# Who forms the sums of a seven-product scheme: accumulating transfers, GpSimd or VectorE, and in which order the pairs come

## The chip, the cores and the metric

One core of a Trainium2 chip runs one layer of a decoder. The metric is device time in microseconds (us) of one execution; the figure for a kernel is the median of several runs.

## The reference, cut to what matters

```python
D_MODEL = 2048; SEQ = 256; N_META = 16; D_FF = 5632      # T = 272 positions
u = rms_norm(h, ffn1_norm_g);  h = h + 0.5 * swiglu(u, w_gate, w_up, w_down)
u = rms_norm(h, mix_norm_g);   z = u @ w_in               # q k v q_idx k_idx w_idx x_c B C gate_attn gate_conv
y_attn = dsa_sparse_attention(q, k, v, q_idx, k_idx, w_idx, k_sel) @ w_attn_branch
y_conv = (gate_b * causal_depthwise_conv(gate_c * x_c, conv_w, conv_b)) @ w_conv_branch
merged = sigmoid(gate_attn) * y_attn + sigmoid(gate_conv) * y_conv
h = h + merged @ w_out
u = rms_norm(h, ffn2_norm_g);  h = h + 0.5 * swiglu(u, w_gate2, w_up2, w_down2)
return h[:, N_META:]
```

All inputs are float32. The kernel gets float32 accuracy by splitting each operand into a high and a low part and multiplying three times (high by high, high by low, low by high).

## The kernel before

**The weight stream.** Every weight is read once from HBM, in the order of use, by the class `Stream`. `load` (L131) issues the transfers on SyncE's queue (SP) into tiles `raw` of 128x2048 floats (1 MB). `split` (L163) cuts a load into subs of at most 128x1024: ScalarE copies a sub into its high part `whi` (L181), VectorE subtracts to get the low part `wlo` (L182). TensorE takes the blocks by `next` (L203). Each time TensorE's program enters a new sub, `next` does four things in this order, and so lays down the order of the instructions on every engine: the `early` functions that are due, the split of the sub that lies `ahead` places further on (3 places in the gates, 5 in the second FFN), the `later` functions that are due (a lag of n means n - 1 subs later), and then the products. There are 3 `raw` tiles up to and with the gates, 4 in the second FFN (`widen`, L124). A `raw` tile can be loaded again when its last sub has been split.

**The stages.** First FFN (to about 790 us of the profile), the mixer's projections, attention and convolution (to about 1086 us), the gates with the two branch products (`gates`, 1086 to 1400), the output projection with `w_out` (1400 to 1478), the second FFN (1478 to the end). The change touches the last three.

**Seven products for eight.** In the gates and in the second FFN, tokens are the stationary side (two blocks of 128 tokens) and 512 weight columns move. A *pair* is two blocks of 128 rows of the sum against two blocks of 512 columns. A pair of kind C is done plainly: eight products of three matmuls each (24 matmuls). A pair of kind S is done as Strassen's method does it: seven products (21 matmuls) into eight PSUM banks `q1` to `q8`, each a 128x512 tile, from sums of weights and sums of tokens. Lists of letters such as `KINDS = "SCSCSCCC"` say which of the eight pairs of a group are C and which are S; a second list says which pair it is.

- Weight sums of an S pair. The five column blocks of a load lie in HBM as a21, a21, a11, a22, a12. SP loads the first two and the next two into one `raw` (L140, L141). GpSimd (POOL) then issues an accumulating transfer that adds a11 and a22 onto the first two (L142), which gives `sa` = (a21 + a11, a21 + a22). The fifth block goes into the small tile `last` (L144; two of these). VectorE forms `sb` in two additions of 128x512 (L159, L160) from `raw` and `last`, in `sum_ahead`, one sub before the pair's first split. The subs of an S pair are "one" (a11, a22), `sa`, `sb`, `last`, of 2, 2, 2 and 1 blocks.
- Token sums of an S pair. `sums_into` (L579) forms four blocks of 128x128 with four instructions on GpSimd; `split_into` (L385) splits the result on ScalarE and VectorE. In the second FFN's down half these are sums of `mid` (tile `more`); `turn_mid` (L1191) puts them, with their split, three lags behind.
- `group` (L617) runs a list of pairs. After the last S pair, `recombine` (L630) puts q1, q5, q6, q7 together in the tiles `va`, `vv`, `vx`, `ve`: one ScalarE copy and four VectorE instructions of 128x512; in a down group four more add the results to `ht` (`after_seven`, L1283). After the last pair, `after_end` adds q3, q2, q4, q8 in that order (L1252 or L1283). A bank can be written by the next group only when its reader here is done. Both come through `early`, so they stand ahead of the splits in VectorE's queue.

**The second FFN's order.** `PLAN` runs four up groups, a down group, four up groups, a down group, three up groups, a down group. An up group makes 512 columns of gate and up. The next group turns its result (`turn_mid`, eight transposes and their split). A down group runs its pairs twice, once for each half of the output columns. So there are eight changes from up group to up group, three from an up to a down group, three from first to second half, and two from a down group to an up group. In up group 0, `norm2` and `turn_h` (transposes of the residual) stand at pair 6.

**Queues.** Each engine's queue is in order. On POOL's queue lie, in the gates and the second FFN, the accumulating transfers, the token sums and some additions of squares (L414).

## Time and profile before

| | |
|---|---|
| median of 3 runs | 2279.72 us (2275.02 to 2285.24) |
| the profiled execution | 2283.87 us; its span from first to last instruction 2282.1 us |
| TensorE busy | 2168.8 us, 95% of the span |
| VectorE busy | 1483.5 us, 65% |
| ScalarE busy | 1085.1 us, 48% |
| GpSimd busy | 125.9 us, 6%, 161 instructions |
| mean granted TensorE clock | 0.979 of full speed |
| HBM read | 439.94 MB |

Times inside the profile count from the first instruction. "Idle before, and what ended it" is given in square brackets behind an instruction; a row of the table of waits gives the total, how often, and the longest. "PEclk" is the share of full clock that TensorE was granted. SPq and POOLq are the queues on which SyncE and GpSimd issue transfers.

### The profile page before, as it was taken

The numbers are of one execution on the slowest core, as the hardware profiler recorded it, in microseconds if no ns is written. First come the engines' busy times: TensorE is split into PE (matmuls) and PEld (weight loads), VectorE is DVE, ScalarE is ACT, GpSimd is POOL, SyncE is SP. The second block draws the span as 40 slices with busy tenths as digits, with TensorE's granted clock in tenths as the row PEclk, the third lists the DMA queues.
The fourth block names the chain that finished last, engine by engine and source line by source line (L and its number), as shares of the span: only waits on it lengthen the run. The fifth ranks groups of instructions, "written<-read, shape, count | busy, mean of one in ns | idle before, by whom it ended". The sixth has DMA issues, their size and how long they took to land. (4 is left out here: it accounts for less than half of the span.)

```text
span 2282.1 us, 32260 instructions
## 1 busy us (share of the span) xinstructions
PE 2168.8 (95%) x13045; PEld 1939.5 (85%) x13045; DVE 1483.5 (65%) x1865; ACT 1085.1 (48%) x1397; POOL 125.9 (6%) x161
## 2 busy tenths in 40 slices
PE   8999999999999999999988999989989999899998
PEld 8999999999999998899866778877767777677776
DVE  7555544555555566875766666777767877678776
ACT  6444433344444454654544444655544555454553
POOL 2000000000000000000200000200000000000010
PEclk9999999999999999999999999999999999999999
DMA  6554555545545545444666654677658776687754
GB/s 240 192 173 178 184 171 181 182 171 183 178 175 184 173 174 170 153 143 166 222 195 192 212 189 169 216 229 226 217 180 251 243 218 215 191 246 239 232 193 139
DMA packets 82517, 444.13 MB, mean 195 GB/s; under 512 B 9184, under 2 KB 9312, under 8 KB 43072
## 3 DMA queue, kind: packets, MB, share of 16 engines
q1 hardware_dynamic: 73584, 410.55, 50.6%
q0 software_dynamic: 8640, 31.35, 8.4%
q8 instruction: 102, 1.67, 0.3%
q14 instruction: 47, 0.39, 0.0%
q10 hardware_dynamic: 144, 0.17, 0.0%
HBM read 439.94 MB, written 2.10 MB: 194 GB/s over the span
## 5 line engine op out<-in xcount | busy, mean ns | idle before, releaser
L182 DVE TENSOR_TENSOR wlo<-raw,whi 128x1024 fp32r<-128x1024 f32 (+1 forms) x752 | 907.8, 1217 | 599.1 <-ACT whi L181 582.9
L181 ACT ACTIVATE whi<-raw 128x1024 fp32r<-128x1024 f32 (+1 forms) x752 | 786.8, 1051 | 868.2 <-PE q L559 185.9
L557 PE MATMUL q<-whi,act 128*128 128x512 f32 x833 | 336.3, 404 | 31.6 <-DVE vx L1252 23.0
L558 PE MATMUL q<-wlo,act 128*128 128x512 f32 x833 | 334.0, 401 | 21.7 <-DVE wlo L182 21.6
L559 PE MATMUL q<-whi,act 128*128 128x512 f32 x833 | 332.4, 399 | 0.0
L557 PEld LDWEIGHTS q<-whi,act 128*128 128x128 f32 x833 | 161.6, 194 | 70.6 <-DVE vx L1252 25.9
L558 PEld LDWEIGHTS q<-wlo,act 128*128 128x128 f32 x833 | 162.3, 195 | 59.3 <-DVE wlo L182 26.0
L351 PE MATMUL pd<-mid,whi 128*128 128x272 f32 x704 | 201.7, 286 | 0.0
L352 PE MATMUL pd<-mid,whi 128*128 128x272 f32 x704 | 201.7, 286 | 0.0
L353 PE MATMUL pd<-mid,wlo 128*128 128x272 f32 x704 | 201.7, 286 | 0.0
L351 PE MATMUL pg<-act,whi 128*128 128x272 f32 x672 | 192.7, 287 | 0.0
L353 PE MATMUL pg<-act,wlo 128*128 128x272 f32 x672 | 192.5, 287 | 0.0
L352 PE MATMUL pg<-act,whi 128*128 128x272 f32 x672 | 192.5, 286 | 0.0
L351 PE MATMUL pu<-act,whi 128*128 128x272 f32 x672 | 192.5, 286 | 0.0
L352 PE MATMUL pu<-act,whi 128*128 128x272 f32 x672 | 192.5, 286 | 0.0
L353 PE MATMUL pu<-act,wlo 128*128 128x272 f32 x672 | 192.5, 286 | 0.0
L559 PEld LDWEIGHTS q<-whi,act 128*128 128x128 f32 x833 | 161.7, 194 | 34.6
L557 PE MATMUL q<-whi,mid 128*128 128x512 f32 x272 | 112.0, 412 | 38.1 <-DVE va L1252 23.9
L351 PEld LDWEIGHTS pd<-mid,whi 128*128 128x128 f32 x704 | 132.6, 188 | 0.0
L352 PEld LDWEIGHTS pd<-mid,whi 128*128 128x128 f32 x704 | 132.6, 188 | 0.0
L353 PEld LDWEIGHTS pd<-mid,wlo 128*128 128x128 f32 x704 | 132.6, 188 | 0.0
L352 PEld LDWEIGHTS pg<-act,whi 128*128 128x128 f32 x672 | 126.6, 188 | 0.0
(286 smaller groups left out, 3792.9 us busy)
## 6 DMA issues: line engine op xcount, KB each, us to landing
raw<-in_wgu_dram SPq DMA_DIRECT2D x87, 1024.0 KB, 4.8
raw<-in_w_dram SPq DMA_DIRECT2D x84, 1024.0 KB, 5.0
raw<-in_w2s_dram SPq DMA_DIRECT2D x96, 512.0 KB, 5.3
raw<-in_wd_dram SPq DMA_DIRECT2D x44, 1024.0 KB, 4.8
raw<-in_wcv_dram SPq DMA_DIRECT2D x24, 1024.0 KB, 4.8
raw<-in_w2s_dram POOLq DMA_DIRECT2D x48, 512.0 KB, 5.8
raw<-in_wg_dram SPq DMA_DIRECT2D x21, 1024.0 KB, 5.9
raw<-in_wb_dram SPq DMA_DIRECT2D x16, 1024.0 KB, 4.8
```

The source lines that it names most:

```text
L181: nc.scalar.activation(to[0], raw, AF.Copy)
L182: nc.vector.tensor_sub(to[1], raw, to[0].bitcast(F32))
L351: nc.tensor.matmul(ps, whi, xhi, start=first, stop=False)
L352: nc.tensor.matmul(ps, whi, xlo, start=False, stop=False)
L353: nc.tensor.matmul(ps, wlo, xhi, start=False, stop=last)
L557: nc.tensor.matmul(ps, xhi, whi, start=n == 0, stop=False)
L558: nc.tensor.matmul(ps, xhi, wlo, start=False, stop=False)
L559: nc.tensor.matmul(ps, xlo, whi, start=False, stop=n == total - 1)
```

## The change

1. Gates: kind S now loads four blocks (a21, a11, a22, a12) in one transfer of 1 MB. VectorE forms `sa` itself in one addition of 128x1024 and then `sb` as before. No accumulating transfer is left there. The gates' groups after the first run their pairs in the order C S S C S C C C (`pairs_gate`).
2. Second FFN: the pairs with an accumulating transfer stay, as kind D. `last` gets three tiles. Down groups run C C D C D C D C (before C C S C S S C C) and C C D C D C (before C C S S C C).
3. Both kinds: the subs come as `sa`, `sb`, one, `last`; the products as q7, q5, q6, q3, q1, q4, q2 (before q1, q4, q7, q5, q6, q3, q2).
4. Token sums are three VectorE instructions in place of four on GpSimd, and sum and split lie at lags of their own (2 and 3, or 3 and 5).
5. `after_end` in the second FFN adds q3, q4, q2, q8. In up group 0, `norm2` and `turn_h` move from pair 6 to pairs 0 to 2; `turn_mid` in a down group uses banks q6 and q1.
6. The pool `tmp` moves to the side that is given back when the residual is.

```diff
-KINDS = "SCSCSCCC"
+KINDS = "DCDCDCCC"
-FIRST = "CCCSCSCC"
+SEVEN = (3, 5, 7)
+def pairs_gate(c):
+    return list(zip("CCCSCSCC", range(PAIRS)) if c == 0 else zip("CSSCSCCC", [0, 3, 5, 1, 7, 2, 4, 6]))
 def pairs_down(gs):
-        kinds, at = "CCSCSSCC", [(0, 2), (1, 2), (0, 0), (2, 2), (1, 0), (2, 0), (3, 0), (3, 2)]
+        kinds, at = "CCDCDCDC", [(0, 2), (1, 2), (0, 0), (2, 2), (1, 0), (3, 0), (2, 0), (3, 2)]
-        kinds, at = "CCSSCC", [(0, 2), (1, 2), (0, 0), (1, 0), (2, 0), (2, 2)]
+        kinds, at = "CCDCDC", [(0, 2), (1, 2), (0, 0), (2, 0), (1, 0), (2, 2)]
...
-            (g, "one", 2 * WIDE, 2, WIDE), (g, "sa", 0, 2, WIDE), (g, "sb", 0, 2, WIDE), (g, "last", 0, 1, WIDE)
+            (g, "sa", 0, 2, WIDE), (g, "sb", 0, 2, WIDE), (g, "one", at * WIDE, 2, WIDE), (g, "last", 3 * WIDE, 1, WIDE)
...
-                last = self.sum_pool.tile([P, WIDE], F32, name="last", tag="last", bufs=2)
+                last = self.sum_pool.tile([P, WIDE], F32, name="last", tag="last", bufs=3)
...
     def sum_ahead(self):
+                if self.seven[g]:
+                    sa, one, last = raw[:, : 2 * WIDE], raw[:, 2 * WIDE : 3 * WIDE], self.sums[g, "last"]
+                else:
+                    add(sa, (raw block 1, raw block 2), (raw block 0, raw block 0))
-                self.nc.vector.tensor_add(sb[:, :WIDE], raw[:, WIDE : 2 * WIDE], raw[:, 2 * WIDE : 3 * WIDE])
-                self.nc.vector.tensor_add(sb[:, WIDE:], sb[:, :WIDE], self.sums[g, "last"])
+                add(sb[:, :WIDE], sa[:, WIDE:], one)
+                add(sb[:, WIDE:], sb[:, :WIDE], last)
...
     def sums_into(t, x):
-        nc.gpsimd.tensor_sub(t[:, 0, :], x[:, 0, :P], x[:, 0, P:])
-        nc.gpsimd.tensor_sub(t[:, 1, :], x[:, 0, P:], x[:, 1, P:])
-        nc.gpsimd.tensor_add(t[:, 2, :], x[:, 1, P:], t[:, 0, :])
-        nc.gpsimd.tensor_sub(t[:, 3, :], x[:, 1, :P], t[:, 2, :])
+        nc.vector.tensor_sub(t[:, :2, :], x[:, 0, :].rearrange("p (j t) -> p j t", j=NT), x[:, :, P:])
+        nc.vector.tensor_add(t[:, 2, :], x[:, 1, P:], t[:, 0, :])
+        nc.vector.tensor_sub(t[:, 3, :], x[:, 1, :P], t[:, 2, :])
...
     def turn_mid(tags):
-            def sums():
-                sums_into(t, x)
-                split_into(two[:, 0, :], two[:, 1, :], t)
-            st.later(sums, 3)
+            st.later(lambda: sums_into(t, x), 3)
+            st.later(lambda: split_into(two[:, 0, :], two[:, 1, :], t), 5)
...
-                    ("q1", b11), ("q4", t4), ("q7", t3), ("q5", t1), ("q6", t2), ("q3", b22), ("q2", b21)
+                    ("q7", t3), ("q5", t1), ("q6", t2), ("q3", b22), ("q1", b11), ("q4", t4), ("q2", b21)
...
-            for tag in ("q3", "q2", "q4", "q8"):
+            for tag in ("q3", "q4", "q2", "q8"):
...
     def up_group(g):                      # g == 0
-                if n >= 6:
-                    for i in range(3) if n == 6 else range(3, 8):
-                        turn_h(i // 2, i % 2, ("q7", "q6", "q5", "q1")[(i - n + 6) % 4 if n > 6 else i])
+                if n < 3:
+                    for i, tag in zip(((0, 1), (2, 3, 4, 5), (6, 7))[n], ("q1", "q5", "q6", "q7")):
+                        turn_h(i // 2, i % 2, tag)
```

## The prediction

> **What bounds the kernel now.** I read the mean clock and the page's busy shares first: TensorE is the bound, so only its stops and its slow stretches can be won. Then I asked for the busy time by stretch, the gates and the second FFN apart, and for TensorE's waits in each.

> ```profile
> 1086.00:1400.00 314.00, 290.58 (x1280) 236.22 (x1279) 200.03 (x223) 148.82 (x171) 19.04 (x24) 0.97 0.60 194
> 1478.00:2283.00 805.00, 725.99 (x3115) 593.77 (x3113) 597.68 (x675) 401.91 (x456) 60.00 (x83) 0.95 0.70 215
> ```

> Length, then busy time of TensorE, weight load, VectorE, ScalarE and GpSimd; then granted clock, share of the DMA engines, GB/s. VectorE has 114 us free in the gates and 207 in the FFN. TensorE's waits (total, times, longest), the two largest of the gates, then five of the FFN:

> ```profile
> PE q L558 <- DVE wlo L182: 18.6, 7, 4.0
> PE q L557 <- DVE va L1131: 3.9, 3, 1.3
> ```
> ```profile
> PE q L557 <- DVE va L1252: 23.9, 3, 10.8
> PE q L557 <- DVE vx L1252: 23.0, 7, 4.8
> PE q L557 <- DVE ht L1283: 18.6, 5, 5.5
> PE pht L1233 <- DVE vx L635: 4.8, 1, 4.8
> PE q L558 <- DVE wlo L182: 3.0, 2, 2.2
> ```

> So 22.5 us of stops in the gates and 73.3 in the FFN. In the FFN 15 of 18 stand at a change of group (L1252, L1283): the first matmul waits for a bank that `after_end` has not emptied. A stop costs clock as well:

> ```profile
> 1774.00:1777.00 3.00, 3.00 (x10) 2.40 (x9) 2.97 (x5) 1.19 (x2) 0.00 (x0) 0.66 0.80 113
> 2170.00:2180.00 10.00, 10.00 (x46) 8.29 (x45) 6.53 (x6) 5.83 (x6) 0.00 (x0) 1.00 0.55 210
> 2203.00:2208.00 5.00, 5.00 (x13) 3.88 (x12) 1.77 (x2) 1.66 (x3) 0.00 (x0) 0.50 0.21 64
> ```

> At full clock 44 whole matmuls take 10 us, 0.227 each (two of the 46 are cut by the edges); behind a stop the clock is 0.50 to 0.66. A C pair is thus 24 x 0.227 = 5.45 us, a seven-product pair 21 x 0.227 = 4.77, one product 0.68. The FFN has 3024 wide matmuls by its loops, 686 us; with some 13 us of transposes and 73.3 of stops, 805 leaves about 32 us lost to low clock, 1.8 for each of 18 stops. In the gates 0.03 x 314 = 9 us is the bound.

> **Part 1: token sums leave GpSimd's queue.** Here is the first change from up to down group, POOL's queue first, then VectorE's, then TensorE:

> ```profile
> 1673.82 0.86 POOL L142 DMA_DIRECT2D raw<-in_w2s_dram  x1 [7.01 <-issue]
> 1674.38 0.78 POOL L582 TENSOR_TENSOR vm<-vm 128x128 f32<-128x128 f32 x1
> ```
> ```profile
> 1666.95 1.22 DVE L182 TENSOR_TENSOR wlo<-raw,whi 128x1024 fp32r<-128x1024 f32 x1 [0.25 <-ACT whi L181]
> 1677.20 0.69 DVE L387 TENSOR_TENSOR more<-vm,more 128x512 fp32r<-128x512 f32 x1 [9.03 <-ACT more L386]
> 1677.81 0.68 DVE L1252 TENSOR_TENSOR vv<-q,vv 128x512 f32<-128x512 f32 x1
> ```
> ```profile
> 1679.24 0.76 PE L557 MATMUL q<-whi,mid 128*128 128x512 f32 x1 [10.76 <-DVE va L1252]
> ```

> An accumulating transfer waits for the plain transfer it adds onto; the token sums stand behind it on POOL, the split of those sums on VectorE waits for them, `after_end` stands behind that split, and TensorE waits for `after_end`. VectorE was free at 1668.17 and TensorE stopped at 1668.48. With the change nothing on VectorE waits for POOL but the weight sums. The three new instructions (one 128x256, two 128x128) have the 128x256 addition as nearest row:

> ```profile
> L182 DVE TENSOR_TENSOR wlo<-raw,whi 128x1024 fp32r<-128x1024 f32 x738 | 898.1, 1227 | 588.5 <-ACT whi L181 576.3 <-PE po L368 0.5
> ...
> L159 DVE TENSOR_TENSOR sb<-raw 128x512 f32<-128x512 f32 x59 | 40.5, 687 | 58.0 <-DMA raw<-in_wgs_dram 46.3 <-DMA raw<-in_w2s_dram 8.6 <-issue 3.0
> ...
> L383 DVE TENSOR_TENSOR h<-h,u 128x256 f32<-128x256 f32 x16 | 6.8, 426 | 8.1 <-ACT u L382 8.1
> ```

> Halving the width from 512 to 256 takes off 0.26, so 128x128 lies between 0.16 and 0.43; I take 0.3, 1.0 us for three, 14 times, 14 us of VectorE's spare time. It counts only ahead of `after_end`.

> *Up to up* (8 changes). `after_end` can start about 0.7 behind TensorE's end (1668.17 + 1.0 against 1668.48), and each of its instructions takes 0.61 back to back. A D pair now comes first and begins with q7, q5, q6, which `recombine` freed pairs ago: nine matmuls, 2.05 us. q3 is then ready at 1.3, q4 at 1.9 (used from 3.4), q2 at 2.5 (from 4.1). No stop, with 0.7 us to spare; the cover is the nine matmuls. The row L1252 `vx` goes, 23.0 us.

> *Up to down* (3). The group begins with C, and C needs q2, which the new order adds third: 0.7 + 3 x 0.61 and a restart of 0.1 to 0.2 are 2.6 us each, 7.8 for 23.9.

> *Up group 0.* The transposes at pairs 0 to 2 use banks that nothing holds, so the 4.8 goes; their cost on TensorE is the same, their eight ScalarE copies lie beside C pairs (ScalarE is 402 of 805 us busy; without that cover the first split of the FFN would be late by them). They also give the second accumulating transfer more time, so the longer of the two waits for L182, 2.2, goes. At the start some 1.2 stays (0.8 of this row and a 0.4 that the view has further down).

> **Part 2: the down groups.** This is VectorE from the last S of a first half, and TensorE's restart:

> ```profile
> 1714.29 0.68 DVE L634 TENSOR_TENSOR vv<-q,va 128x512 f32<-128x512 f32 x1
> ...
> 1719.34 2.35 DVE L182 TENSOR_TENSOR wlo<-raw,whi 128x1024 fp32r<-128x1024 f32 x2
> 1722.70 0.69 DVE L159 TENSOR_TENSOR sb<-raw 128x512 f32<-128x512 f32 x1 [1.00 <-DMA raw<-in_w2s_dram]
> ...
> 1724.04 2.35 DVE L182 TENSOR_TENSOR wlo<-raw,whi 128x1024 fp32r<-128x1024 f32 x2
> 1726.31 2.48 DVE L1283 SCALAR_TENSOR_TENSOR ht<-q,ht 128x512 f32<-128x512 f32 x4
> ```
> ```profile
> 1727.73 0.76 PE L557 MATMUL q<-whi,mid 128*128 128x512 f32 x1 [4.17 <-DVE ht L1283]
> 1773.67 0.50 PE L557 MATMUL q<-whi,act 128*128 128x512 f32 x1 [2.19 <-DVE ht L1283]
> ```

> TensorE stopped at 1723.56; two C pairs (10.9) before that the last S ended, at 1712.66. `recombine` began 1.63 later and ran with `after_seven` for 5.05; four splits (4.6), the next sums (1.34) and 1.0 of waiting follow, then `after_end`. In the new order only one C pair stands behind the last D. In *first to second half* (3), 1.63 + 5.05 + two splits 2.3 + sums 1.34 = 10.3 against 5.45 of cover: `after_end` starts 4.9 late, q2 is third (1.85), and with 0.2 to restart (1727.73 against two additions from 1726.31) the stop is 6.9 each, 20.7 in all, where it is now 4 to 5.5. This step goes against the change. In *down to up* (2), 1.63 + 5.05 + 1.75 (a split of 512, one of 1024) - 5.45 = 3.0, q3 at 3.6 against nine matmuls: 1.7 each where the second row has 2.19. At the very end `recombine` finishes 1.2 behind TensorE and four additions follow, 2.5 us more than now.

> FFN: now 73.3 + 32 = 105; then 1.2 + 7.8 + 20.7 + 3.4 = 33.1 of stops, 8 x 1.8 + 0.5 = 15 of clock, 2.5 at the end: 51. Gain 54. Bounds of this step: every boundary as now but without the waits for POOL gives 60, halves at 9 each give 45. The third `last` tile frees only SP's queue, `tmp` on the other side moves no instruction, and `turn_mid`'s new banks are free since `recombine`: I give these nothing, as no stop is charged to them. The two token sums of the output projection (2 us) lie beside its matmuls.

> **Part 3: the gates.** Issues with KB each and median time to landing, and VectorE's wait there:

> ```profile
> raw<-in_wg_dram SPq DMA_DIRECT2D x21, 1024.0 KB, 5.9
> ...
> raw<-in_wgs_dram SPq DMA_DIRECT2D x22, 512.0 KB, 4.1
> ...
> raw<-in_wgs_dram POOLq DMA_DIRECT2D x11, 512.0 KB, 7.5
> ```
> ```profile
> DVE sb L159 <- DMA raw<-in_wgs_dram: 46.3, 11, 6.4
> ```

> An S pair's sums need 4.1 and then 7.5; after the change one transfer of 5.9, with two issues fewer on SP's queue, none on POOL's, and 0.75 MB less to move. With three `raw` tiles that is the wait of 4.2 a pair behind L182's 18.6. The added 128x1024 addition is 1.23 by the row of `wlo` (between 0.69 and 1.23 by width), 11 times, 14 us of the 114 free. On the path: two S pairs in a row need 2 x (2.6 of sums + 4.1 of splits) = 13.4 on VectorE against 9.5, behind the merge's six instructions (3.7) and with a C pair (5.45) of lead. Through the queue from TensorE's entry into the group: merge to 3.7, two splits to 6.0, the second S's sums to 8.6, the first S's 512-wide split to 9.2. Only then is its tile loaded for the third S: landed at 15.1, summed at 17.7, and the C split behind that at 18.9, which TensorE wants at 17.7 (C, S, S and half a C). So 1.2 stays for each of three groups. C first uses q2 and q3, free since the branch, so the wait for the merge (L1131, 3.9) goes. Gates: 22.5 + 9 becomes 4 + 1.5, gain 26.

> **Sum.** 54 + 26 = 80. The profiled execution is 2283.87, 4 us above the median of the runs, well within their spread: 2204 against it, 2200 for the median.

> [...] In the row from 1774 the clock fell behind a stop of 2.19. [...]

> [...]

> [...]

> **The rivals.**
> - *VectorE's queue takes half of it back* (0.20). `after_end` starts a split later than I have it (1.2 us, over the spare 0.7) at the eight up changes, and the gates keep half of their stops. 8 x (0.5 to 1.5 + 1.8) = 18 to 26, plus 13: 2231 to 2239. For it: VectorE's work per group does not shrink.
> - *Less is left than I have it* (0.08). If sums and splits at the halves run ahead of `recombine`, 3 x 3.6 come off, 2189; if short stops cost no clock, 9 come off, 2191; both 2180. Against it: the order of the program, and the row from 1774.
> - *GpSimd only looked guilty* (0.08): behind it VectorE's own backlog holds `after_end`, as at 1726.31. The FFN stays, only the gates' 26 are won, the halves lose 8: 2262.
> - *Slower* (0.06): `sa` is first in a D pair, so the accumulated half is wanted two products (1.36 us) earlier. If each of the 48 transfers is just in time now, that is 65 us of stops, and at 1 us of clock each (half of what a stop costs now, as they are short) 48 more: 2200 + 113 = 2313. It decides from 1.7 us a pair (80 / 48). Against it: the sums, which stand ahead of all subs in VectorE's queue, need the same half already, and only 8.6 us of their wait (L159) is charged to these transfers.

> **How the numbers follow.** The forecast has 0.58, 2186 to 2222 by itself. The range takes in the first two rivals: 2178 to 2243. No change is within 0.5%, 11 us. Faster: 0.58 + 0.20 + 0.08 and half of the third, 0.90; same 0.05; slower 0.05.

> **What would show it.** The waits for L1252 `vx` and L1131 gone; VectorE never waiting for `more`; three stops of about 7 us at the changes of half and three near 2.6 into a down group; FFN clock 0.97 to 0.98; gates near 287 us. I am wrong if VectorE waits for `raw` in most D pairs, or if the up groups keep stops over 1 us.

## The result, and the profile after

The changed kernel takes 2196.88 us (median of four runs, 2194.66 to 2201.74) beside 2277.37 us for the kernel before: a ratio of 0.9644, 95% interval 0.9612 to 0.9676. Its profiled execution took 2201.74 us, the longest of the four, with a span of 2200.0, so the span is 82.1 us shorter.

Where the time went is cleanest between three marks: the first matmul of the gates, the first of the second FFN, the end. From the timeline, TensorE (start, length, line, operation), before and then after:

```profile
1086.76 0.40 PE L557 MATMUL q<-whi,act 128*128 128x512 f32 x1
1470.21 0.40 PE L557 MATMUL q<-whi,act 128*128 128x512 f32 x1
```
```profile
1086.60 0.40 PE L577 MATMUL q<-whi,act 128*128 128x512 f32 x1
1436.47 0.40 PE L577 MATMUL q<-whi,act 128*128 128x512 f32 x1
```

Gates and output projection went from 383.5 to 349.9 us, 33.6 won; the second FFN, to the end of the span, from 811.9 to 763.5, 48.4 won. The stages before the gates are unchanged. By the matmuls the projection starts at 1378.03 and the FFN at 1470.21 in the kernel before, not at 1400 and 1478; all of the 33.6 lies in the gates, as the projection takes 92.2 us in both kernels. Busy time by stretch after the change, columns as in the prediction (the first stretch holds the gates and the start of the projection, the second the FFN without its first 8.5 us):

```profile
1086.00:1400.00 314.00, 311.88 (x1461) 260.26 (x1460) 238.35 (x279) 167.12 (x205) 3.85 (x4) 1.00 0.54 190
1445.00:2201.00 756.00, 709.52 (x3108) 583.25 (x3106) 599.94 (x700) 395.63 (x454) 41.05 (x47) 0.97 0.74 229
```

In the gates TensorE is busy 311.88 of 314 us at full clock, where it had 290.58 at 0.97. VectorE does more there (238.35 for 200.03) and it does not matter. TensorE's waits after the change, those of the FFN and then the only two left in the gates and the projection:

```profile
PE q L577 <- DVE ht L1301: 23.9, 5, 6.8
PE q L577 <- DVE va L1270: 9.4, 3, 4.2
...
PE q L577 <- DVE vv L1270: 4.1, 2, 2.7
PE pht L1251 <- ACT ht L1252: 2.5, 1, 2.5
```
```profile
PE po L386 <- ACT whi L202: 1.3, 2, 0.7
PE q L578 <- DVE wlo L203: 0.8, 1, 0.8
```

`after_end` is now L1270 (up) and L1301 (down), the split L202 and L203. The row `vx` (23.0 us in seven waits) is gone. The FFN's stops are 40.3 us with one of 0.4 that the rows above leave out, where they were 73.7 (73.3 and one of 0.4). One of each kind, in order of time:

```profile
1575.78 0.50 PE L577 MATMUL q<-whi,act 128*128 128x512 f32 x1 [1.42 <-DVE vv L1270]
1619.05 0.47 PE L577 MATMUL q<-whi,mid 128*128 128x512 f32 x1 [2.62 <-DVE va L1270]
1670.09 0.76 PE L577 MATMUL q<-whi,mid 128*128 128x512 f32 x1 [6.83 <-DVE ht L1301]
1717.50 0.50 PE L577 MATMUL q<-whi,act 128*128 128x512 f32 x1 [1.69 <-DVE ht L1301]
1847.42 0.50 PE L577 MATMUL q<-whi,act 128*128 128x512 f32 x1 [2.67 <-DVE vv L1270]
2119.36 0.77 PE L577 MATMUL q<-whi,mid 128*128 128x512 f32 x1 [4.19 <-DVE va L1270]
```

The first and the fifth are two of the three stops left at a change from up to up group (the third is the one of 0.4, for a copy on ScalarE); the second and the sixth stand into a down group; the third is a change of half (three of them, 6.83 each), the fourth a change from down to up (two, 1.69 each).

### The profile page after: what moved, and what is told of

Same layout as the page of the kernel before. It is cut to its first block, busy times and chain, and to the rows that moved or that the text cites. A ratio compares the mean times of both kernels' runs of the same rounds, so it can differ in the third digit from the quotient of the medians.

```text
span 2200.0 us, 32155 instructions
## 1 busy us (share of the span) xinstructions
PE 2143.0 (97%) x13045; PEld 1926.7 (88%) x13045; DVE 1503.8 (68%) x1918; ACT 1080.3 (49%) x1397; POOL 82.3 (4%) x94
## 4 chain that ended last, share of the span: by engine, by line
PE 85%; DVE 8%; ACT 2%; DMA 2%; issue 1%; POOL 1%; SPq 0%; DVEq 0%; ACTq 0%; POOLq 0%
PE q L577 11%; PE q L578 11%; PE q L579 11%; PE pd L372 4%; PE pd L371 4%; PE pd L373 4%; PE pu L371 4%; PE pg L371 4%; PE pg L373 4%; PE pu L373 4%; PE pu L372 4%; PE pg L372 4%; DVE wlo L203 3%; DMA raw<-in_w2d_dram 2%; ACT whi L202 2%; PE po L386 1%
## 5 line engine op out<-in xcount | busy, mean ns | idle before, releaser
L203 DVE TENSOR_TENSOR wlo<-raw,whi 128x1024 fp32r<-128x1024 f32 (+1 forms) x752 | 903.7, 1208 | 607.5 <-ACT whi L202 591.2
L202 ACT ACTIVATE whi<-raw 128x1024 fp32r<-128x1024 f32 (+1 forms) x752 | 782.8, 1044 | 858.8 <-PE q L579 187.8
L577 PE MATMUL q<-whi,act 128*128 128x512 f32 x833 | 327.1, 393 | 8.0 <-DVE vv L1270 4.1
L578 PE MATMUL q<-wlo,act 128*128 128x512 f32 x833 | 325.5, 391 | 0.8 <-DVE wlo L203 0.8
L579 PE MATMUL q<-whi,act 128*128 128x512 f32 x833 | 325.0, 390 | 0.0
L577 PEld LDWEIGHTS q<-whi,act 128*128 128x128 f32 x833 | 157.0, 188 | 42.5 <-DVE vv L1270 5.4
L578 PEld LDWEIGHTS q<-wlo,act 128*128 128x128 f32 x833 | 157.0, 188 | 33.6 <-DVE wlo L203 1.9
L579 PEld LDWEIGHTS q<-whi,act 128*128 128x128 f32 x833 | 156.9, 188 | 32.9
## 6 DMA issues: line engine op xcount, KB each, us to landing
raw<-in_wgu_dram SPq DMA_DIRECT2D x87, 1024.0 KB, 4.8
raw<-in_w_dram SPq DMA_DIRECT2D x84, 1024.0 KB, 5.0
raw<-in_w2d_dram SPq DMA_DIRECT2D x96, 512.0 KB, 5.5
raw<-in_wd_dram SPq DMA_DIRECT2D x44, 1024.0 KB, 4.8
raw<-in_wg_dram SPq DMA_DIRECT2D x32, 1024.0 KB, 4.8
raw<-in_wcv_dram SPq DMA_DIRECT2D x24, 1024.0 KB, 4.8
raw<-in_w2d_dram POOLq DMA_DIRECT2D x48, 512.0 KB, 5.7
raw<-in_wb_dram SPq DMA_DIRECT2D x16, 1024.0 KB, 4.9
```

What stands on the lines that cost most here:

```text
L202: nc.scalar.activation(to[0], raw, AF.Copy)
L203: nc.vector.tensor_sub(to[1], raw, to[0].bitcast(F32))
L577: nc.tensor.matmul(ps, xhi, whi, start=n == 0, stop=False)
L578: nc.tensor.matmul(ps, xhi, wlo, start=False, stop=False)
L579: nc.tensor.matmul(ps, xlo, whi, start=False, stop=n == total - 1)
```

## The experiments

Ratios are to the kernel before, measured beside each run on the same chip. Beside these runs it took 2275.4 to 2280.6 us (medians), so a difference of a few us between two runs is at the edge of what their times alone can tell.

### Token sums: is it the engine or the place?

The change does two things to the token sums of the down groups: it moves them from GpSimd to VectorE, and it takes their split from the lag of the sums (3) to a later one (5), which puts that split behind `after_end` in VectorE's queue. Each was undone alone, then both.

e1, the sums back on GpSimd, the lags as changed:

```diff
-        nc.vector.tensor_sub(t[:, :2, :], x[:, 0, :].rearrange("p (j t) -> p j t", j=NT), x[:, :, P:])
-        nc.vector.tensor_add(t[:, 2, :], ...); nc.vector.tensor_sub(t[:, 3, :], ...)
+        nc.gpsimd.tensor_sub(t[:, 0, :], x[:, 0, :P], x[:, 0, P:])   # and the other three, as before
```

> Token sums back on GpSimd (four instructions), everything else as changed: the split of the sums still lies two subs behind them. Queue theory (TensorE stops because after_end stands in VectorE's queue behind a split that waits for POOL's queue): that split now stands behind after_end, so nothing is held; stops from up to up group as in the changed kernel or smaller (VectorE has 1.0 us less ahead of after_end), 2190 to 2202 us. Rival (GpSimd itself is too slow or too late for these sums): VectorE waits for `more` again by some 4 us eight times, 2225 to 2240 us.

e2, the sums on VectorE, with their split at lag 3:

```diff
-            st.later(lambda: split_into(two[:, 0, :], two[:, 1, :], t), 5)
+            st.later(lambda: split_into(two[:, 0, :], two[:, 1, :], t), 3)
```

> Token sums on VectorE, but sum and split at the same lag, as before the change, in the second FFN's down half. Queue theory: the split's VectorE half waits about 1 us for ScalarE and takes 0.6, all ahead of after_end: stops near 1 us appear at the eight changes from up to up group, and those into a down group grow by 1.6; 2208 to 2220 us. Rival (only the engine matters): no change, 2194 to 2200.

e3, both edits:

> Token sums on GpSimd and sum and split at the same lag: the whole token-sum part undone, the orders kept. Queue theory: VectorE's wait for `more` returns (about 30 us in all), the stops into a down group return to about 10, 10 and 3 us, those from up to up group to 1.5 to 2.5 us, less than before because q7, q5, q6 come first; 2232 to 2252 us. Rival (the order of products alone cured the changes of group): 2197 to 2212.

| sums on | split behind `after_end` (lag 5) | split ahead of it (lag 3) |
|---|---|---|
| VectorE | 2196.88, 0.9644 [0.9612, 0.9676] (the change) | 2210.61, 0.9694 [0.9676, 0.9712] (e2) |
| GpSimd | 2190.49, 0.9606 [0.9585, 0.9626] (e1) | 2228.0, 0.977 [0.9751, 0.9789] (e3) |

The place decides more than the engine. Putting the split late is worth 13.7 us with the sums on VectorE and 37.5 with them on GpSimd. The engine is worth 17.4 us with the split early, where VectorE waits for GpSimd as before. With the split late GpSimd's queue costs nothing here, and the sums on VectorE are if anything 6 us dearer (the two intervals overlap). In e2, as expected, VectorE waits 0.7 us for `more` at eight places and the stops into a down group are 4.00 each, where the regular ones of the change are 2.62; of the eight changes from up to up, five stop, for 0.68 to 2.94. e3 has the old chain again, in small. VectorE's total wait for `more` there, then from the timeline POOL, VectorE, and TensorE's restart at a change from up to up group:

```profile
DVE more L407 <- ACT more L406: 25.0, 8, 4.6
```
```profile
1583.09 0.86 POOL L149 DMA_DIRECT2D raw<-in_w2d_dram  x1 [9.09 <-DVE wlo L203]
1583.65 0.79 POOL L602 TENSOR_TENSOR vm<-vm 128x128 f32<-128x128 f32 x1
...
1586.50 0.69 DVE L407 TENSOR_TENSOR more<-vm,more 128x512 fp32r<-128x512 f32 x1 [3.40 <-ACT more L406]
...
1587.85 0.50 PE L577 MATMUL q<-whi,act 128*128 128x512 f32 x1 [2.40 <-DVE vv L1271]
```

The sums start on POOL only behind the issue of a transfer, VectorE idles 3.40 us for their split, and `after_end` starts behind it, at 1587.11. In e1, with the sums in the same queue, one wait for `more` of 1.0 us is left, and it stands behind `after_end`. e3 came 4 us better than the lower end of what was expected: its stops into the down groups were 4.28, 4.28 and 4.69, not 10, 10 and 3. Its five stops from up to up were 1.87 to 4.39, longer than the 1.5 to 2.5 expected.

e1's stops at the changes of group are also smaller than the change's: into a down group 5.4 us for 9.4 and from up to up 0.2 for 4.5. Its stops at the FFN's start are longer by 2.9 (two for a split, 1.3, and the transposes' wait for ScalarE 4.1 for 2.5), so in sum 34.9 us stay of 40.3. So the three additions on VectorE are not hidden where `after_end` is already late; the sizes are worked out under "Up to up" below.

In e1 the four sums, all of one shape, differ on GpSimd by more than half in their mean (the slowest and the quickest in the FFN; count, then busy time in us and mean in ns):

```profile
L603 POOL TENSOR_TENSOR vm<-vm 128x128 f32<-128x128 f32 x9 | 10.2, 1137 | 0.0
...
L605 POOL TENSOR_TENSOR vm<-vm,vm 128x128 f32<-128x128 f32 x9 | 6.2, 689 | 0.7
```

No run here shows why, and in e1, with the split late, it cost nothing that the times show (2190.49 us for the change's 2196.88).

### Order of products and subs

e4, the change with the products as q1, q4, q7, q5, q6, q3, q2, the subs as one, `sa`, `sb`, and `after_end` as q3, q2, q4, q8 again:

```diff
-                    ("q7", t3), ("q5", t1), ("q6", t2), ("q3", b22), ("q1", b11), ("q4", t4), ("q2", b21)
+                    ("q1", b11), ("q4", t4), ("q7", t3), ("q5", t1), ("q6", t2), ("q3", b22), ("q2", b21)
```

> Products q1, q4, q7, q5, q6, q3, q2, subs one, sa, sb, last, and after_end in the order q3, q2, q4, q8, as before the change; sums stay on VectorE in steps. Queue theory with cover: q4 is wanted after one product (0.68 us) and is added third: stops near 2 us at the eight changes from up to up group and 4 into an up group from a down group; into a down group and between halves 0.6 less each; 2212 to 2230 us. Rival (the order does nothing, only the sums' place does): 2190 to 2200.

Measured: 2212.08 us, ratio 0.9699 [0.9681, 0.9717], 15 us worse than the change. The `vx` row is back, eight waits at the eight changes from up to up:

```profile
PE q L577 <- DVE vx L1270: 12.8, 8, 1.8
```

As expected, the two stops from a down to an up group grow (4.25 each for 1.69), and those between halves (6.23 for 6.83) and into a down group (2.02 for 2.62) shrink by 0.6 each. So `vx` had two causes: GpSimd's chain made it up to 4.8 us long, and the old product order, which wants q4 with its second product, left 0.86 to 1.85 even without that chain. Nine matmuls on free banks are the cover, as the prediction had it. In the gates the product order is worth nothing: the projection starts at 1344.49 in e4 and at 1344.30 in the change.

### The gates: one transfer or the order?

e5 keeps the new order C S S C S C C C and goes back to five blocks with an accumulating transfer:

```diff
-zip("CCCSCSCC", range(PAIRS)) if c == 0 else zip("CSSCSCCC", ...)
+zip("CCCDCDCC", range(PAIRS)) if c == 0 else zip("CDDCDCCC", ...)    # and wg in two kinds of load
```

> Gates with the accumulating transfers of before (kind D, five blocks a load), in the changed order C D D C D C C C and with sums on VectorE; second FFN as changed. Transfer theory: VectorE waits for `raw` in the gates again, near 4 us a pair, and TensorE's waits for L182's line return to 15 to 25 us plus clock: 2215 to 2230 us. Rival (the order of the gates' pairs won it): gates stay within 5 us, 2194 to 2204.

e6 keeps the single transfer and goes back to the order S C S C S C C C:

```diff
-zip("CSSCSCCC", [0, 3, 5, 1, 7, 2, 4, 6])
+zip("SCSCSCCC", [3, 0, 5, 1, 7, 2, 4, 6])
```

> Gates in the old order S C S C S C C C with the new single transfers. Transfer theory: only the wait for the merge returns, some 1.5 us at each of three groups, and the adjacent S pairs' load on VectorE goes: 2196 to 2204 us. Rival (order): the waits for the splits come back too, 2212 to 2225.

e10 undoes both:

> The changed kernel with both parts of the gates undone: five-part accumulating transfers and the order of before (an S pair first, then C, S, C, S, C, C, C). Theory (either cure alone removes the waits for a split: the order gives the accumulated tile two C pairs of lead, the single transfer needs none): the split waits come back, some 12 to 19 us of them, beside the merge waits of 6.7 that the old order has with single transfers (2208.8 there); 2208.8 plus 12 to 19 and its clock: 2221 to 2236. Rival (the split waits of before came from the old product order, q1 first, or from the token sums in the projection, which stay changed here): 2206 to 2213, split waits under 2 us.

| transfer | order C S S C S C C C | order S C S C S C C C |
|---|---|---|
| single, sums on VectorE | 2196.88, 0.9644 [0.9612, 0.9676] (the change) | 2208.8, 0.969 [0.9674, 0.9707] (e6) |
| accumulating | 2197.38, 0.9639 [0.962, 0.9657] (e5) | 2231.3, 0.9807 [0.9781, 0.9833] (e10) |

The start of the FFN in e5, e6 and e10 (the gates start at 1086.5 in all three), each with TensorE's waits in the gates:

```profile
1440.01 0.40 PE L578 MATMUL q<-whi,act 128*128 128x512 f32 x1
...
PE q L579 <- DVE wlo L203: 2.7, 4, 1.9
...
DVE sb L180 <- DMA raw<-in_wgd_dram: 9.9, 4, 5.0
```
```profile
1448.77 0.40 PE L577 MATMUL q<-whi,act 128*128 128x512 f32 x1
...
PE q L577 <- DVE ve L1152: 6.7, 3, 2.2
```
```profile
1470.25 0.40 PE L578 MATMUL q<-whi,act 128*128 128x512 f32 x1
...
PE q L579 <- DVE wlo L203: 14.9, 4, 5.7
PE q L578 <- DVE ve L1153: 9.3, 3, 3.1
...
DVE sb L180 <- DMA raw<-in_wgd_dram: 41.0, 9, 7.1
```

Gates and projection take 353.5 (e5), 362.3 (e6) and 383.7 us (e10), against 349.9 with the change and 383.5 before. e10, as expected, gives the old stage back to a fraction of a us although the new product order and VectorE's token sums stay in it: together they are worth nothing there (the waits move, 14.9 for a split and 9.3 for the merge, where before they were 18.6 and some 4). Against e10 the order alone brings 30.2 us, the single transfer alone 21.4, both 33.8; they are not a sum, because both remove the same waits for a split. With the order alone VectorE's wait for the accumulated half falls from 41.0 to 9.9. The single transfer leaves VectorE nothing to wait for (e6). Only the order removes the wait for the merge of the group before (L1152), because C starts on q2 and q3. e5's expectation was missed by 18 us and its rival held; e6 fell between its two, its split waits gone, its merge waits there.

### The down groups

The prediction said that ending a half on one C pair behind the last D goes against the change. e7 puts the D pairs of a down group back as they were:

```diff
-        kinds, at = "CCDCDCDC", ... ;  "CCDCDC", ...
+        kinds, at = "CCDCDDCC", ... ;  "CCDDCC", ...
```

> Down groups in the old order of kinds (C C D C D D C C; C C D D C C), all else as changed. By my working the change's own order costs: with two C pairs behind the last D the stop between halves is 3.8 to 5.5 us in place of 6.8, the one into the next up group goes (1.7), and the end is 2.5 us shorter: 2183 to 2191 us. Rival (the later D spreads VectorE's work and helps): stops between halves as they are or longer, 2197 to 2210.

2188.53 us, ratio 0.9602 [0.9587, 0.9617], 8 us better than the change and as expected. The stops at the halves shrink to 4.71, 5.02 and 6.21 and those into an up group go, for longer waits of VectorE for the accumulated half (14.5 us in five with the change), since two D pairs in a row want two of them:

```profile
DVE sb L180 <- DMA raw<-in_w2d_dram: 19.0, 10, 3.4
```

e8 goes on from there: each half gets an order for what stands at its border. Half 0 ends on two C pairs as in e7; half 1 starts with a D pair, whose first nine matmuls use banks long free, and ends on three C pairs, so `recombine` is done before the end; ahead of a down group `after_end` adds q2 first, which the C pair there needs.

```diff
+            ("CCDCDDCC", [(0, 2), (1, 2), (0, 0), (2, 2), (1, 0), (2, 0), (3, 0), (3, 2)]),   # half 0
+            ("DCDCDCCC", [(0, 0), (0, 2), (1, 0), (1, 2), (2, 0), (2, 2), (3, 0), (3, 2)]),   # half 1
-            for tag in ("q3", "q4", "q2", "q8"):
+            for tag in ("q2", "q3", "q4", "q8") if g == part[g][-1] else ("q3", "q4", "q2", "q8"):
```

> An order for each half: the first half keeps C C first and ends on two C pairs, the second half begins with D and ends on three C pairs (two in the short group: D C D C C C); ahead of a down group after_end adds q2 first. Theory: a D that comes first needs no bank for nine matmuls (2.05 us), and with 10.9 us of C pairs behind the last D after_end starts on time: no stop between halves (3 x 6.8) nor into an up group (2 x 1.7), 1.4 to 3 into a down group: 2155 to 2170 us. Rival (VectorE's work or the accumulating transfers bind there): stops of 2 to 4 us remain between halves and new waits of VectorE for `raw` appear, 2174 to 2188.

2157.35 us (2154.7 to 2160.1), ratio 0.9463 [0.9447, 0.9479]: some 40 us under the change and better than both kernels. Busy time of the FFN, and TensorE's waits in it:

```profile
1440.00:2150.00 710.00, 699.62 (x3124) 578.54 (x3124) 598.51 (x702) 398.15 (x459) 42.40 (x49) 1.00 0.79 243
```
```profile
PE q L583 <- DVE va L1276: 4.3, 3, 1.4
PE q L583 <- DVE vv L1276: 3.2, 3, 2.3
PE pht L1257 <- ACT ht L1258: 2.9, 1, 2.9
```

No stop is left between halves or into an up group, 10.4 us remain of 40.3, and the clock of the FFN is 1.00 for 0.97. The FFN is now close to its matmuls alone: of 710 us TensorE is busy 699.62. e8 makes three edits at once, and no run takes them apart; that e7, with the first of them in both halves, won only 8 us suggests that most lies in the other two.

e9 is e8 with the token sums on GpSimd in their steps, which had been worth 6 us in e1:

> The order per half of the kernel before this one, and in it the token sums back on GpSimd in their steps. Theory (the sums cost VectorE about 1.0 us a pair wherever after_end or a weight sum is late, so they took back 6 us at the change's own orders, 2196.9 against 2190.5; the orders and the sums are separate costs): 2157.4 minus 6, 2151, range 2147 to 2155; the irregular stops at up to up (2.34 is the largest) fall under 0.5. Rival (the up groups' stops are set by the late accumulated transfers alone, and GpSimd's sums, queued behind the issues of those transfers, come late where VectorE needs them): 2156 to 2164, with VectorE waiting for `more` again.

A miss: 2158.19 us, ratio 0.9482 [0.9462, 0.9502], no different from e8, within the rival's range. Its waits of TensorE in the FFN:

```profile
PE pht L1258 <- ACT ht L1259: 3.8, 1, 3.8
PE pt L631 <- DVE vm L1284: 2.3, 2, 1.2
PE q L583 <- DVE va L1277: 1.6, 3, 0.7
```

The stops meant did shrink ("va" from 4.3 to 1.6; from up to up one of 0.5 is left of 3.2), but `turn_mid`'s transposes now wait 2.3 for VectorE, `pht` 0.9 longer, and two splits at the FFN's start 1.3. In sum 9.4 us of stops for 10.4. The transposes' wait is the rival's: in the first two down groups the sums start on POOL only behind the issue of an accumulating transfer (1623.51), VectorE waits 2.4 us for their split, and the products that the transposes read (L1284) stand behind that split. Here is the first of the two:

```profile
1627.54 0.69 DVE L413 TENSOR_TENSOR more<-vm,more 128x512 fp32r<-128x512 f32 x1 [2.39 <-ACT more L412]
1628.27 0.75 DVE L1284 SCALAR_TENSOR_TENSOR vm<-vx,r,va 128x512 f32<-128x512 f32 x1
```

So a late split is free on GpSimd only as long as nothing that TensorE soon wants stands behind it. Most of what the move wins at the changes of group (5.4 us) it loses here and at the FFN's start (4.5).

## Why the prediction was right, and where its steps were off

- **Sum.** 80 us were predicted for the profiled execution and 82.1 came. That it fits so well is luck, out of two errors that cancel: the FFN gave 48.4 for 54, the gates and the projection 33.6 for 26. Part of the FFN's shortfall is this execution's own: the same FFN takes 758 to 759 us in e5, e6 and e10, where here it took 763.5.
- **Halves, down to up, into a down group.** 6.9, 1.7 and 2.6 were predicted, 6.83, 1.69 and 2.62 measured. Counting VectorE's queue instruction by instruction, with durations of the page of the profile, held to 0.1 us at the regular stops of these three kinds, where nothing in that queue waits for a transfer.
- **Up to up: no stop predicted, 4.5 us measured** in three stops, and the third into a down group 4.19 for 2.6. Two of the three, 1.42 and 2.67, are over the 1 us that the prediction itself named as a sign of being wrong. This is the term that was mis-sized: the spare 0.7 us was counted on a VectorE that never waits, while the `sb` additions still wait for a late accumulated half. VectorE ahead of the stop at 1575.78:

```profile
1562.74 0.69 DVE L180 TENSOR_TENSOR sb<-raw 128x512 f32<-128x512 f32 x1 [3.33 <-DMA raw<-in_w2d_dram]
...
1574.05 0.42 DVE L602 TENSOR_TENSOR vm<-vm 128x256 f32<-128x256 f32 x1
...
1574.83 0.29 DVE L604 TENSOR_TENSOR vm<-vm,vm 128x128 f32<-128x128 f32 x1
1575.04 0.68 DVE L1270 TENSOR_TENSOR vv<-q,vv 128x512 f32<-128x512 f32 x1
```

  The token sums (1.0 us in all, as estimated) stand between the late half and `after_end`. The chain of waits goes through a transfer of 9.05, 11.45 and 9.78 us ahead of the three irregular stops (at 1575.78, 1847.42 and 2119.36), and through none ahead of the regular ones. VectorE's waits for it in the FFN:

```profile
DVE sb L180 <- DMA raw<-in_w2d_dram: 14.5, 5, 5.3
```

  No run took these transfers' delay away by itself, but it varies from run to run, and the stop follows it. VectorE's wait for the late half, and TensorE's stop some 13 us later at a change from up to up:

| run | sums on | wait for the half, us | stop, us | wait less stop |
|---|---|---|---|---|
| the change | VectorE | 3.33 | 1.42 | 1.91 |
| e5 | VectorE | 3.43, 2.14 | 1.52, 0.23 | 1.91, 1.91 |
| e6 | VectorE | 2.72, 3.43, 2.67 | 0.82, 1.55, 0.76 | 1.90, 1.88, 1.91 |
| e7 | VectorE | 3.43, 3.20 | 1.53, 1.29 | 1.90, 1.91 |
| e8 | VectorE | 4.24, 2.32, 2.27 | 2.34, 0.46, 0.37 | 1.90, 1.86, 1.90 |
| e10 | VectorE | 2.53, 3.75, 2.49 | 0.64, 1.84, 0.57 | 1.89, 1.91, 1.92 |
| e1, e9 | GpSimd | 3.04, 3.40 | 0.16, 0.51 | 2.88, 2.89 |

  With the sums on VectorE the queue takes up 1.9 us of a late half, and what is beyond that stops TensorE; without them it takes up 2.9. The difference is the 1.0 us of the three additions. So at up to up both parts of the cause are shown; why these transfers land late stays open, and for the stop at 2119.36 only the chain of waits speaks. (At the change's longest wait, 5.28, the stop is 2.67 behind the one of 0.41. In up groups that turn no result, the first behind a down group, there is more slack: a wait of 2.29 in e7 stopped nothing.) The prediction saw this wait's row (8.6 us before) and let it stand only as a condition of the slower rival.
- **Up group 0.** 1.2 us at the start was predicted and 2.5 came, as a wait of another kind. "The transposes at pairs 0 to 2 use banks that nothing holds" was wrong for pair 1: it takes q1 and q5 again, and ScalarE's copies of what pair 0 put there start only at 1447.56, behind splits in ScalarE's queue.
- **Clock and end.** 33.4 of the FFN's 48.4 us are stops (40.2 were predicted), so 15.0 came from clock and end, where 17 less 2.5 was predicted. The end cost 0.7 in place of 2.5: the additions of `after_seven` were done 1.0 us ahead of TensorE's end (2193.9 and 2194.9), not behind it. That leaves 15.7 for the clock. The granted clock itself gives 30.4 us lost before and 15.8 after (half of TensorE's busy time at 0.50), about 14.7 won. The prediction's 32 for the loss before came near that although its 805 us leave out the FFN's first 7.8; so near was luck.
- **Gates.** 4 us of stops were expected to stay, 0.8 did. The third S tile was charged a landing of 5.9 us, the row of before; after the change loads of 1 MB from the same tensor land in 4.8 (median of 32), which takes the 1.2 per group to 0.1. It is not the end of the accumulating transfers that made them quicker: e5 keeps those and has 4.9. So 22.5 us of stops were won for 18.5, and 11.1 beside the stops for the 7.5 that were put down to the clock; the granted clock shows 7.1 of them, and where the other 4 come from is open. The credit was also too narrow: "with three `raw` tiles that is the wait of 4.2 a pair behind L182's 18.6" is true of the transfer (e6 has no such waits but the 0.8), but the order, credited with the 3.9 of the merge alone, removes nearly all of them too (e5).
- **"Token sums leave GpSimd's queue."** The chain was read rightly and its links were all there (e3 has them again). But of the two edits that cut it, the prediction credited the move to VectorE; e1 shows that the later split does it alone, and that the move then wins nothing. The move alone (e2) cuts less. In a chain of four links it is enough to cut one.
- **Product order.** The nine matmuls as cover were right: without them 12.8 us of `vx` remain (e4).
- **The rivals.** VectorE's queue did take something back, as the first rival had it, but 4.5 us of stops from up to up and not 31 to 39 us. "Short stops cost no clock" (its 9 us are 1.8 for each of five stops, three of 2.6 and two of 1.7) held for the two of 1.69, with a granted clock of 1.00 in the 3 us of the restart, and not for those of 2.62 and 2.61, with 0.59 and 0.60. GpSimd did not only look guilty: e3 brings 25.0 us of waits for its sums back. "`sa` first" did not cost: VectorE waits for `raw` in 5 of 48 D pairs.
- **Not tested.** No run undoes the third `last` tile, the moved pool, `turn_mid`'s banks or the new place of up group 0's transposes by itself.

## What to carry to other kernels

Before moving work off an engine that seems late, look for what stands *behind* the wait in the waiting engine's queue: putting the waiting instruction behind the one that frees the bank may be enough (e1: 2190.49 us where e3 has 2228.0), and costs nothing on another engine, as long as nothing that is wanted soon stands behind it there (e9: no gain, 2158.19 us for 2157.35). At every border of a stage, let the work that begins use resources free for long (here a pair that starts on three unused banks), and let the work that ends leave its last long chain two pairs earlier; the two halves of one loop may need different orders. When a change contains two cures of one wait, their gains are not a sum: undo each alone and both.

## What the runs showed of the hardware that was not expected

```profile
1715.14:1718.55 3.41, 1.72 (x8) 1.08 (x8) 3.41 (x5) 1.06 (x1) 0.87 (x1) 1.00 0.72 202
1718.55:1721.96 3.41, 3.41 (x17) 2.82 (x16) 3.37 (x6) 1.28 (x2) 0.00 (x0) 1.00 0.69 130
```
```profile
2098.48:2101.89 3.41, 1.54 (x8) 0.94 (x7) 2.16 (x4) 0.63 (x1) 0.48 (x2) 1.00 0.71 127
2101.89:2105.30 3.41, 3.41 (x10) 2.63 (x9) 2.95 (x5) 3.04 (x4) 0.00 (x0) 0.50 0.00 0
1583.05:1586.46 3.41, 2.40 (x11) 1.66 (x9) 0.04 (x1) 0.62 (x1) 2.63 (x5) 1.00 0.69 136
1586.46:1589.88 3.42, 2.03 (x9) 1.67 (x10) 3.38 (x6) 0.86 (x3) 0.00 (x0) 1.00 0.43 84
1589.88:1593.29 3.41, 3.41 (x17) 2.81 (x16) 2.94 (x4) 3.41 (x5) 0.00 (x0) 1.00 0.00 0
```

A step with 1.69 us idle left the clock at 1.00, one with 1.87 took it to 0.50 for the whole next step, and 2.40 spread over two steps (1.01 and 1.39) cost nothing. From the gates to the end, all twelve profiled runs together have 3765 steps that stood at full clock. In 97 of them TensorE was idle for 1.84 us or more, and each was followed by a step at 0.50; in the other 3668 it was idle for at most 1.79, and none was. (The kernel before and the change alone: 26 steps with 2.10 us or more, 607 with at most 1.69.) A step at half clock costs up to 1.7 us, half of 3.41. That is near the 1.8 that the prediction charged to every stop, right for those of 2.6 and too much for those of 1.7.
